# Modulation blocks behind their bank's products, bias rows loaded at a pair's start, and one product step ahead of the second group's scores

## The chip, the cores and the metric

One core of a Trainium2 chip runs the kernel as one program. The metric is the device time of one execution in microseconds (us). Engines: TensorE (PE in the profile, PEld its weight loads), VectorE (DVE), ScalarE (ACT), GpSimd (POOL) and SyncE (SP), which here issues nearly all DMAs.

## The reference

One layer of a hybrid diffusion model over T = 640 tokens (512 of a sample on an 8 by 64 grid, 128 of a prompt), width 1024:

```python
q_a, k_a, v_a, q_b, k_b, v_b = project(modulate(rmsnorm(x), shift, scale), w_in)
o_a = neighborhood_attn(q_a, k_a, v_a, cache_a_k, cache_a_v, rpb)      # 8 heads, 8x16 window, bias rpb
o_b = window_attn(rope_2d(q_b), rope_2d(k_b), v_b, cache_b..., sink)   # 8 heads, 2 kv heads
x = x + gate1 * rmsnorm(concat(rmsnorm(o_a), rmsnorm(o_b)) @ w_out)
x = x + gate2 * rmsnorm(conv_ffn(modulate(rmsnorm(x), shift2, scale2)))
shift, scale, gate1, shift2, scale2, gate2 = split(silu(c) @ w_mod + b_mod, 6)
```

This is a shortened form. The prompt's tokens attend to each other in full with the same weights, and their keys and values are outputs too. The modulation is 48 column blocks of 128: 24 of them are wanted only after attention.

## The kernel before, in words

All products are made of float32 operands split into a high and a low part, so each product of 128 by 128 weights is three matmuls (`mm3`, all recorded at line 127, in `mm`). In the same way `tt` (L111) stands for all two-operand passes and `act` (L108) for all passes of ACT.

**Stages.** Norms, transposes, the first modulation columns and V run to about 64 us in an order written by hand. From there to about 343 us the attention runs, and in that region a scheduler of the tile framework orders each engine's instructions from its own cost estimates; the source only gives the order of the program. Then the output projection and the feed-forward follow, by hand again.

**The attention region.** A software pipeline, `Pipe.slot` (L872), takes a list of jobs: for each of four head pairs p four tiles of neighbourhood attention and one of the prompt, then for each of four groups g the window attention. A job makes scores in a bank `psS` (two banks), a softmax (`soft1`, L620: a DVE pass at L626 adds the bias table `tab` and finds the extreme `nm`, writing a tile `P`; ACT takes the exponent), transposes of P (`psT`) and products with V (`psO`). Between the jobs' steps `fill_run` (L855) lets PE work on projections that a later job needs, for so many us as it is given: `qk_gen` (L584) makes query and key of the next pair, `qb_gen` (L1008) the rotated query of the next group, `kb_gen` and `vb_gen` the window's key and value.

**A bank and its block.** Each projection goes through `tgemm` (L542): 24 products of 128 x 320 (8 steps k of three) gather in columns 0 to 320 of a bank `psg`; there are two such banks. Columns 320 to 450 hold one modulation block at the same time, made by `side_gen` (L824) in four stages: (1) eight matmuls with a block of 128 columns of `w_mod`, tile `wms` (L371, in `ada_mm`); (2) a copy T by ACT, and `side_load` (L817), which starts the next `wms` of 512 KB on SP's queue into the one buffer there is; (3) a product of T with `sel` on PE (L835), which sums four row groups; (4) DVE adds the bias and puts the column into S, G or another table. 24 blocks go with 24 banks. What reads a finished bank (q, k, the rotation) is put on the list `pend`, and `flush` (L537) emits it at k = 1 of the next `tgemm`.

**Bias tables.** The relative-position bias of a head is loaded in four DMAs from a scratch tensor (`load_traw`, L242, on SP's queue) into a tile `traw`, from which POOL copies seven pieces into `tab` (`tab_ops`, L490, recorded at L505). `traw` and the P tiles are of one pool with eight buffers (L59). `pre_natten(p)` (L1180) puts the loads and the copies of the next pair's two heads on `bg`, a list from which each slot takes four entries. SP also loads the projection weights (`wst`, L338) and the cached keys and values (`cc`, L442 and L443), whose buffers come from a pool that the outgoing prompt keys (`ko`) use as well.

**Before the windows.** `pre_window(g)` (L1195) empties the fill list and puts the next group's query on it; the slots have 4.4 us each for the pairs and 4.2 for the groups.

Of the kernel before, what the change touches and what calls it, by code (L numbers as in the profile page):

```python
# [26 lines left out]
def trunk_kernel(  # L27
# [46 lines left out]
    def U(shape, name, dt=F32):  # L74
        return up_.tile(shape, dt, tag="u", name=name)
# [8 lines left out]
    def PB(shape, name, dt=F32):  # L84
        return pp_.tile(shape, dt, tag="p", name=name)
# [4 lines left out]
    def QT(shape, name, dt=F32):  # L90
        return qp_.tile(shape, dt, tag="q", name=name)
# [9 lines left out]
    def PS(kind, name):  # L101
        return PSB[kind].tile([128, 512], F32, tag=kind, name=name)
# [19 lines left out]
    def split(hi, lo, src):  # L122
        act(hi, src)
        tt(lo, src, f(hi), ALU.subtract)
# [4 lines left out]
    def mm3(out, lh, ll, rh, rl, start, stop):  # L129
        mm(out, lh, rh, start, False)  # L130
        mm(out, lh, rl, False, False)
        mm(out, ll, rh, False, stop)
# [109 lines left out]
    def load_traw(h):  # L242
        traw[h] = t = PB([128, 2, 256], f"traw{h}")
        for v in range(2):
            for jj in range(2):
                sv = scr[v, h]
                nc.sync.dma_start(
                    out=t[jj * 64:jj * 64 + 64, v, :],
                    in_=bass.AP(tensor=sv.tensor, offset=sv.offset + jj * 8, ap=[[32, 8], [1, 8], [1, 256]]))
# [130 lines left out]
    def hh(k, lo, s):  # L380
        return (hL if lo else hH)[k // 4][:, k % 4, s]
# [150 lines left out]
        for h_, l_, s_ in parts:  # L532
            tt(l_, s_, f(h_), ALU.subtract)

    pend = []

    def flush():  # L537
        now, pend[:] = pend[:], []
        for fn in now:
            fn()  # L540

    def tgemm(w, ch):  # L542


        wh, wl = w
        ps_ = PS("g", "psg")
        s_ = slice(ch * 320, ch * 320 + 320)
        sd = side_gen(ps_[:, 320:450], m128)
        yield next(sd, 0.0)
        for k in range(KD):  # L550
            mm3(ps_[:, 0:320], wh[:, k, :], wl[:, k, :], hh(k, 0, s_), hh(k, 1, s_), k == 0, k == KD - 1)
            if k == 1:
                flush()
            if ch and k == 3 and stream.nt > 1:
                stream.split()
            yield 0.41 + (next(sd, 0.0) if k in (2, 7) else 0.0)
        pend.append(lambda: next(sd, 0.0))
        return ps_

    RW = [slice(0, 64), slice(64, 128)]  # L560
# [23 lines left out]
    def qk_gen(p):  # L584
        q = QT([128, 2, T], f"q{p}", F32R)
        if p:
            load_cc(p)
        cc = CC.pop(p)
        w = stream.take()
        ps0 = yield from tgemm(w, 0)  # L590
        pend.append(lambda: split(q[:, 0, 0:320], q[:, 1, 0:320], ps0[:, 0:320]))
        ps1 = yield from tgemm(w, 1)
        pend.append(lambda: split(q[:, 0, 320:640], q[:, 1, 320:640], ps1[:, 0:320]))
        ku = U([128, 2576], f"k{p}", F32R)
        kt = ku[:, 0:2304].rearrange("p (e c) -> p e c", e=2)
        vc = ku[:, 2304:2560].rearrange("p (h s d) -> p h s d", h=2, s=2)
        QK[p] = (q, kt, vc)

        def part(o, src):
            n = src.shape[-1]  # L600
            return kt[:, 0, o:o + n], kt[:, 1, o:o + n], src

        w = stream.take()
        pt = PS("t", "pst")
        nc.tensor.transpose(pt[:, 0:128], cc[:, 0], ident)
        pend.append(lambda: k_ctx(kt, pt[:, 0:128], 448, 3))
        pend.append(lambda: split(vc[:, :, 0, :], vc[:, :, 1, :], cc[:, 1].rearrange("p (h d) -> p h d", h=2)))
        ps2 = yield from tgemm(w, 0)
        pend.append(lambda: splits(part(128, ps2[:, 0:320]), part(576, ps2[:, 192:320])))
        ps3 = yield from tgemm(w, 1)  # L610

        def last():
            splits(part(704, ps3[:, 0:192]), part(1024, ps3[:, 192:320]))
            nc.vector.tensor_copy(cc[:, 2], ps3[:, 192:320])
            pend.append(lambda: prompt_k_out(cc[:, 2], nak[:, p * 128:p * 128 + 128]))

        pend.append(last)
# [206 lines left out]
    def side_gen(ps_, m_, ahead=True):  # L824
        if not sides:
            return
        cb, w = sides.pop(0)
        what, k = cb // 8, cb % 8
        ada_mm(ps_, lambda k_: w[:, k_, :], 0, 128)
        yield 0.5  # L830
        act(m_, ps_[:, 0:128])
        if ahead:
            side_load()
        yield 0.0
        nc.tensor.matmul(ps_[:, 128:130], m_, sel[:, 0:2], start=True, stop=True, skip_group_check=True)  # L835
        yield 0.11
        bb = T1[:, W_MODT + cb:W_MODT + cb + 1].to_broadcast([128, 2])
        if what == 3:
            tt(S2[:, k, :], ps_[:, 128:130], bb, ALU.add)
        else:  # L840
            tmp = SM([128, 2], "gtmp")
            tt(tmp, ps_[:, 128:130], bb, ALU.add)
            if what == 4:
                ts(G2[:, k, :], tmp, 1.0, T1[:, W_GF + k:W_GF + k + 1], ALU.add, ALU.mult)
            else:
                gc = (W_GMP if what == 2 else W_GFP) + k
                ts((G1 if what == 2 else S1)[:, k, :], tmp, T1[:, gc:gc + 1], None, ALU.mult)
        yield 0.0
# [6 lines left out]
    def fill_run(us, last=None):  # L855

        carry[0] += us
        while fill and carry[0] > 0:
            try:
                d = next(fill[0][1])  # L860
                if d is None:
                    break
                carry[0] -= d
            except StopIteration:
                name = fill.pop(0)[0]
                if last is not None and name == last:
                    break
        carry[0] = min(carry[0], 0.0)

    bg = []  # L870
# [56 lines left out]
    def rope(src, o, n, dH, dL):  # L927

        mask = [i ^ 16 for i in range(32)]
        rx = FP([128, 2, 320], "rx")  # L930
        x_, sh = rx[:, 0, 0:n], rx[:, 1, 0:n]
        tt(x_, src, cs[:, 0, o:o + n], ALU.mult)
        nc.vector.stream_shuffle(sh, src, mask)
        tt(sh, sh, cs[:, 1, o:o + n], ALU.mult)
        tt(x_, x_, sh, ALU.add)
        js = slice(o // 64, (o + n) // 64)
        split(jview(dH)[:, js], jview(dL)[:, js], x_.rearrange("p (j r c) -> p j r c", r=8, c=8))
# [70 lines left out]
    def qb_gen(g):  # L1008
        q = QB[g] = QT([128, 2, T], f"qb{g}", F32R)
        w = stream.take()  # L1010
        p0 = yield from tgemm(w, 0)
        dH, dL = q[:, 0, 0:512], q[:, 1, 0:512]
        pend.append(lambda: rope(p0[:, 0:320], 0, 320, dH, dL))
        p1 = yield from tgemm(w, 1)

        def last():
            rope(p1[:, 0:192], 320, 192, dH, dL)
            split(q[:, 0, 512:640], q[:, 1, 512:640], p1[:, 192:320])

        pend.append(last)  # L1020
# [97 lines left out]
    def run_ops(ops):  # L1118
        for fn in ops:
            fn()  # L1120
# [59 lines left out]
    def pre_natten(p):  # L1180
        def run():
            fill_run(1e9)
            flush()
            if p < 3:
                fill.append((f"qk{p + 1}", qk_gen(p + 1)))
                for h in (2 * p + 2, 2 * p + 3):
                    bg.append(lambda h=h: load_traw(h))
                    bg.extend(tab_ops(h, (nc.gpsimd,)))
            else:
                fill.append(("kb", kb_gen()))  # L1190
                fill.append(("vb", vb_gen()))
                fill.append(("qb0", qb_gen(0)))
        return run

    def pre_window(g):  # L1195
        def run():
            fill_run(1e9)
            for _ in range(4 if g == 0 else 1):
                flush()
            if g == 0:  # L1200
                ob_.extend(U([128, 4, T], f"ob{i}", F32R) for i in range(2))
            if g == 2:
                wa[0, 0], ops = load_wo(0, 0, 0, wr_, 0)
                bg.extend(ops)
            if g == 3:
                wa[0, 1], ops = load_wo(0, 0, 1, wr_, 0)
                run_ops(ops)
                for i in range(2):
                    wa[1, i], ops = load_wo(0, 1, i, None, 0)
                    bg.extend(ops)  # L1210
            if g < 3:
                fill.append((f"qb{g + 1}", qb_gen(g + 1)))
            else:
                fill.append(("wa0", wa_gen(0)))
        return run
# [784 lines left out]
```

## Time and profile before

| | us |
|---|---|
| median of 3 runs (848.74 to 855.26) | 848.97 |
| profiled execution | 855.52 |
| its span | 853.6 |
| PE busy | 806.5 (94%) |
| DVE, ACT, POOL busy | 564.7, 436.0, 303.2 |
| mean granted clock of TensorE | 0.976 |

A row of the page names a line, an engine, an operation and its tiles, out<-in. In a row of the timeline the bracket at the end holds the idle time just before the instruction and what ended it. A row of the waits gives an engine, its tile and line, what it waited for, the total, the count and the longest. The granted clock is the share of full speed that TensorE was allowed in a stretch.

### The profile page before, as it was taken

How to read it: one execution, taken by the hardware profiler on the slowest of the kernel's cores; microseconds unless marked ns; L12 is line 12 of the kernel's file. 1: busy time of each engine (PE TensorE's matmuls, PEld its weight loads, DVE VectorE, ACT ScalarE, POOL GpSimd, SP SyncE). 2: the span in 40 equal slices, each digit the busy share in tenths (PEclk: the TensorE clock that was granted, in tenths of full speed). 3: DMA queues.
4: the chain of work that ended last, by engine and by line, in shares of the span. 5: the costliest groups of instructions: out<-in, count | busy, mean ns of one | idle time of the engine just before them, and what ended most of it. 6: DMA issues, size and time to landing. Idle time of an engine off the chain costs nothing.

```text
span 853.6 us, 13902 instructions
## 1 busy us (share of the span) xinstructions
PE 806.5 (94%) x5304; PEld 708.5 (83%) x5304; DVE 564.7 (66%) x1023; ACT 436.0 (51%) x876; POOL 303.2 (36%) x352
## 2 busy tenths in 40 slices
PE   6999989899999999989997999999999999999996
PEld 5679778788777777768997999999999987888885
DVE  3455555555888875676679899898898864332115
ACT  5345665645667886465445545546456544332112
POOL 3452333323221211346964466575575200000002
PEclk8999999999999999999998999999999999999999
DMA  9954535436312113567124243233332436434313
GB/s 290 277 142 127 155 97 142 122 105 164 86 50 75 50 51 104 197 207 196 42 65 128 83 129 110 87 115 104 107 115 84 125 114 221 171 110 161 114 50 124
DMA packets 140158, 106.59 MB, mean 125 GB/s; under 512 B 12560, under 2 KB 121388, under 8 KB 140092
## 3 DMA queue, kind: packets, MB, share of 16 engines
q1 hardware_dynamic: 139084, 105.05, 41.5%
q8 instruction: 42, 0.69, 0.4%
q10 hardware_dynamic: 1008, 0.66, 0.3%
q14 instruction: 24, 0.20, 0.1%
HBM read 92.53 MB, written 13.16 MB: 124 GB/s over the span
## 4 chain that ended last, share of the span: by engine, by line
PE 48%; DVE 28%; ACT 7%; DMA 5%; issue 4%; POOL 4%; SPq 1%; DVEq 0%; ACTq 0%; POOLq 0%
PE psd L127 16%; PE psg L127 8%; DVE cv L120 7%; DVE ou L111 5%; PE psv L127 4%; DVE cv L111 3%; DVE owl L111 3%; PE zx L127 3%; POOL fg L111 3%; PE psya L127 3%; PE psyb L127 2%; DMA wms<-in_w_mod_dram 2%; PE psS L127 2%; ACT cv L108 2%; DVE yy L111 2%
## 5 line engine op out<-in xcount | busy, mean ns | idle before, releaser
L127 PE MATMUL psd<-dwh,a 128*128 128x512 f32 x440 | 138.3, 395 | 0.0
L111 POOL TENSOR_TENSOR wsum<-wraw 128x512 f32<-128x512 f32 x36 | 77.2, 2166 | 96.9 <-DVE oc L111 89.1
L127 PE MATMUL zx<-h2H,ou 128*128 128x322 f32 x392 | 96.7, 316 | 7.5 <-DVE cv L120 4.4
L127 PEld LDWEIGHTS psd<-dwh,a 128*128 128x128 f32 x440 | 82.9, 188 | 19.7
L127 PE MATMUL psd<-dwl,a 128*128 128x512 f32 x220 | 87.1, 396 | 0.1
L111 DVE TENSOR_TENSOR dwl<-wd,dwh 128x1024 fp32r<-128x1024 f32 x22 | 26.9, 1224 | 86.7 <-ACT dwh L108 86.7
L127 PE MATMUL psg<-hH,wh 128*128 128x320 f32 x224 | 76.0, 339 | 4.4 <-ACT T L108 4.2
L127 PEld LDWEIGHTS zx<-h2H,ou 128*128 128x128 f32 x392 | 69.0, 192 | 9.9 <-DVE yy L111 5.2
L127 PE MATMUL psg<-hH,wl 128*128 128x320 f32 x224 | 70.5, 315 | 0.0
L127 PE MATMUL psg<-hL,wh 128*128 128x320 f32 x224 | 70.3, 314 | 0.0
L108 ACT ACTIVATE dwh<-wd 128x1024 fp32r<-128x1024 f32 x22 | 23.3, 1060 | 91.4 <-PE psd L127 85.7
L117 POOL TENSOR_SCALAR rdv<-ssdc 128x1 f32<-128x1 f32 x5 | 1.6, 329 | 177.3 <-ACT jk L108 177.3
L127 PE MATMUL zx<-h2L,ou 128*128 128x322 f32 x196 | 61.4, 313 | 0.0
L127 PEld LDWEIGHTS psg<-hH,wh 128*128 128x128 f32 x224 | 42.8, 191 | 13.2 <-ACT T L108 7.9
L108 ACT ACTIVATE cv<-yy,T 128x642 f32<-128x642 f32 x20 | 17.7, 886 | 66.1 <-DVE yy L111 66.1
L127 PEld LDWEIGHTS psd<-dwl,a 128*128 128x128 f32 x220 | 41.3, 188 | 10.4 <-DVE dwl L111 0.6
L111 POOL TENSOR_TENSOR wl<-wst,wh 128x1024 fp32r<-128x1024 f32 (+1 forms) x12 | 27.7, 2311 | 58.5 <-ACT wh L108 41.7
L120 DVE SCALAR_TENSOR_TENSOR cv<-yy,T,cv 128x641 f32<-128x641 f32 x40 | 35.4, 884 | 17.9 <-ACT cv L108 17.2
L108 ACT ACTIVATE P<-P,nm 128x320 f32<-128x320 f32 (+3 forms) x64 | 40.3, 630 | 7.0 <-DVE nm L626 6.9
L127 PEld LDWEIGHTS psg<-hL,wh 128*128 128x128 f32 x224 | 43.1, 192 | 0.5
L127 PEld LDWEIGHTS psg<-hH,wl 128*128 128x128 f32 x224 | 42.9, 192 | 0.0
L108 ACT ACTIVATE cv<-cv 128x642 f32<-128x642 f32 x22 | 16.4, 744 | 50.2 <-DVE cv L120 50.2
(354 smaller groups left out, 2248.0 us busy)
## 6 DMA issues: line engine op xcount, KB each, us to landing
wraw<-in_w_up_dram SPq DMA_DIRECT2D x40, 512.0 KB
wms<-in_w_mod_dram SPq DMA_DIRECT2D x32, 512.0 KB
wd<-in_w_down_dram SPq DMA_DIRECT2D x22, 512.0 KB
wm<-in_w_mod_dram SPq DMA_DIRECT2D x16, 512.0 KB
aD<-cv SPq DMA_DIRECT2D x22, 321.0 KB
ar<-aD SPq DMA_DIRECT2D x11, 642.0 KB
wst<-in_w_in_dram SPq DMA_DIRECT2D x10, 512.0 KB
yD<-Y SPq DMA_DIRECT2D x5, 512.0 KB
```

Source lines behind the costliest of these rows:

```text
L108: return nc.scalar.activation(out=out, in_=in_, func=func, **kw)
L111: return (eng or nc.vector).tensor_tensor(out=out, in0=a, in1=b, op=op)
L117: return e.tensor_scalar(out=out, in0=a, scalar1=s1, scalar2=s2, op0=op0, op1=op1)
L120: return nc.vector.scalar_tensor_tensor(out=out, in0=a, scalar=s, in1=b, op0=op0, op1=op1)
L127: return nc.tensor.matmul(out, l, r, start=start, stop=stop, skip_group_check=True, **kw)
```

## The change

Three edits, all in the attention region. New lines shift the numbers below the first one by up to six: the sel product is L835 before and L841 after, `side_load`'s DMA L821 and L827, the transposes L708 and L714.

1. `tgemm` makes its block's eight matmuls behind its 24 products instead of ahead of them. The copy T goes on `pend` (so it is emitted at k = 1 of the next `tgemm`, as the first reader of the bank, together with the next `wms` load), sel comes at k = 4 of the next `tgemm`, and DVE's bias add is put on `pend` there. The last block's rest is emitted in `pre_window(3)`.
2. `pre_natten` calls `load_traw` for both heads of the next pair at once, at the start of the pair; only the copies stay on `bg`.
3. `pre_window(0)` runs the fill list for 2.0 us more right after the second group's query has been put on it.

```diff
 def tgemm(w, ch):
     sd = side_gen(ps_[:, 320:450], m128)
-    yield next(sd, 0.0)
     for k in range(KD):
         mm3(ps_[:, 0:320], ...)
         if k == 1:
             flush()
...
-        yield 0.41 + (next(sd, 0.0) if k in (2, 7) else 0.0)
+        late = 0.0
+        if k == 4 and side_late:
+            late = next(side_late[0], 0.0)
+            pend.append(lambda g=side_late.pop(): next(g, 0.0))
+        yield 0.41 + late
+    yield next(sd, 0.0)
     pend.append(lambda: next(sd, 0.0))
+    side_late.append(sd)
     return ps_
...
 def pre_natten(p):
             for h in (2 * p + 2, 2 * p + 3):
-                bg.append(lambda h=h: load_traw(h))
+                load_traw(h)
                 bg.extend(tab_ops(h, (nc.gpsimd,)))
...
 def pre_window(g):
+            if g == 3:
+                for g_ in side_late:
+                    next(g_, 0.0)
+                    next(g_, 0.0)
...
             if g < 3:
                 fill.append((f"qb{g + 1}", qb_gen(g + 1)))
+                if g == 0:
+                    fill_run(2.0)
```

How the scheduler's order moves. On PE, at the second block (hH and hL are the split activations, wh and wl the split weights, k_872 and q_807 the pair's keys and queries); before:

```order
L127 MATMUL psg<-hH_573,wl 128x320
L835 MATMUL psg<-sel,T_99 128x2
L127 MATMUL psS<-k_872,q_807 128x384 x3
L371 MATMUL psg<-wms,cpad 32x128 x8
L127 MATMUL psg<-hH_174,wh 128x320
L127 MATMUL psg<-hL_175,wh 128x320
L127 MATMUL psg<-hH_174,wl 128x320
```

and now, at the first and the second block:

```order
L127 MATMUL psg<-hH_573,wl 128x320
L371 MATMUL psg<-wms,cpad 32x128 x8
L127 MATMUL psg<-hH_174,wh 128x320
L127 MATMUL psg<-hL_175,wh 128x320
L127 MATMUL psg<-hH_174,wl 128x320
L127 MATMUL psS<-k_872,q_807 128x384 x6
...
L127 MATMUL psg<-hH_573,wl 128x320
L841 MATMUL psg<-sel,T_99 128x2
L127 MATMUL psg<-hH_573,wh 128x320
...
L371 MATMUL psg<-wms,cpad 32x128 x8
L127 MATMUL psS<-k_872,q_807 128x384 x6
```

The sel product stood at its bank's end, next to the following block; now it stands 15 products behind the block, in the following bank, with 9 more products from there to the next block. The group of six scores, which was split into three and more, stands whole. In the whole region PE changes from one kind of work to another 273 times, 306 before. Of the 24 sel products none carried a wait before; now 14 carry one for DVE and 17 one for ACT. Of the products of psg 26 waited for ACT and 3 for DVE; now it is 2 and 24.

On SP's queue, from the first pair on; before:

```order
L247 DMA traw_984<-scr 64x1x256 x4
L821 DMA wms<-in_w_mod_dram 128x8x128
L338 DMA wst<-in_w_in_dram 128x8x128 x2
L821 DMA wms<-in_w_mod_dram 128x8x128
L442 DMA cc<-in_cache_a_k_dram 128x128
L443 DMA cc<-in_cache_a_v_dram 128x128
L442 DMA cc<-in_cache_a_k_dram 128x128
L443 DMA cc<-in_cache_a_v_dram 128x128
L338 DMA wst<-in_w_in_dram 128x8x128
L821 DMA wms<-in_w_mod_dram 128x8x128
L247 DMA traw_1135<-scr 64x1x256 x4
```

and now:

```order
L247 DMA traw_975<-scr 64x1x256 x4
L827 DMA wms<-in_w_mod_dram 128x8x128
L247 DMA traw_981<-scr 64x1x256 x4
L338 DMA wst<-in_w_in_dram 128x8x128 x2
L442 DMA cc<-in_cache_a_k_dram 128x128
L443 DMA cc<-in_cache_a_v_dram 128x128
L442 DMA cc<-in_cache_a_k_dram 128x128
L827 DMA wms<-in_w_mod_dram 128x8x128
L338 DMA wst<-in_w_in_dram 128x8x128
L443 DMA cc<-in_cache_a_v_dram 128x128
L827 DMA wms<-in_w_mod_dram 128x8x128
```

The second head's rows (traw_1135, now traw_981) stood behind four cache loads and now stand ahead of all of them; the second `wms` load stood ahead of the cache loads and now stands behind three of them.

On PE, before the first scores of the windows (kvU the window's keys, qb_2645 and qb_2638 the rotated query); before:

```order
L835 MATMUL psg<-sel,T_99 128x2
L995 MATMUL pstb<-ident,vbT 128x128
L708 MATMUL psT<-ident,P 128x128 x3
L371 MATMUL psg<-wms,cpad 32x128 x8
L127 MATMUL psg<-hH_174,wh 128x320
...
L127 MATMUL psg<-hH_174,wl 128x320
L127 MATMUL psS<-kvU,qb_2645 128x384 x6
L708 MATMUL psT<-ident,P 128x128 x3
```

and now:

```order
L127 MATMUL psg<-hH_573,wl 128x320
L841 MATMUL psg<-sel,T_99 128x2
L714 MATMUL psT<-ident,P 128x128 x4
L127 MATMUL psS<-kvU,qb_2638 128x384 x6
L714 MATMUL psT<-ident,P 128x128 x2
L127 MATMUL psg<-hH_573,wh 128x320
```

Nine products of the second group's query stood between the last block and the window's first scores, and now fifteen stand between the last projection and these scores, with sel behind them; nine more products follow before the next block, and the transposes of P, six in all, are four ahead and two behind.

More of the change, by code (lines that the diff above doesn't have):

```diff
@@ L533, in splits @@
             tt(l_, s_, f(h_), ALU.subtract)
-    pend = []
+    pend, side_late = [], []
     def flush():
```

## The prediction

> **What bounds the kernel now.** I read the busy times first, then the table of stretches, the waits of TensorE (PE), the chain that ended last, and single rows around each wait.
>
> ```profile
> PE 806.5 (94%) x5304; PEld 708.5 (83%) x5304; DVE 564.7 (66%) x1023; ACT 436.0 (51%) x876; POOL 303.2 (36%) x352
> PE   6999989899999999989997999999999999999996
> ```
>
> PE sets the end: busy for 806.5 of 853.6 us, and nearly full in every slice. Moving work on another engine pays only where PE stood idle for it. All three edits lie between 64 and 343 us. The next view sums the waits of PE from 78 to 330 us (line, what it waited for, us in total, times, longest).
>
> ```profile
> PE psg L127 <- ACT T L108: 4.2, 7, 1.1
> PE psS L127 <- DVE nm L626: 3.0, 2, 1.5
> PE psg L371 <- DMA wms<-in_w_mod_dram: 2.1, 3, 0.8
> PE psS L127 <- ACT qb L108: 1.8, 1, 1.8
> ...
> PEld psg L127 <- ACT T L108: 7.9, 14, 1.4
> ```
>
> These four groups of PE, 4.2 + 3.0 + 2.1 + 1.8 = 11.1 us, are what the change can touch. PEld counts the first of them as 7.9, because a weight load starts its wait while the matmul ahead still runs. Two stretches hold something more than waiting (columns: length, busy of PE, PEld, DVE, ACT, POOL, granted clock, DMA share, GB/s):
>
> ```profile
> 117.00:122.60 5.60, 4.14 (x42) 3.28 (x37) 2.78 (x9) 3.07 (x9) 2.37 (x6) 1.00 0.62 140
> 122.60:127.00 4.40, 3.89 (x16) 3.00 (x17) 2.26 (x8) 2.34 (x8) 1.75 (x6) 0.64 0.01 2
> 127.00:150.00 23.00, 23.00 (x191) 19.95 (x190) 12.65 (x45) 14.18 (x39) 8.44 (x19) 0.99 0.50 135
> 150.00:156.10 6.10, 4.63 (x47) 3.75 (x45) 2.41 (x7) 3.22 (x8) 2.22 (x6) 1.00 0.61 131
> 156.10:161.00 4.90, 4.20 (x21) 3.89 (x22) 3.56 (x13) 3.80 (x12) 3.52 (x8) 0.69 0.00 0
> ```
>
> After each of the two stalls that end at 122.6 and 156.1 the granted clock is 0.64 and 0.69 for more than 4 us; between them it is 0.99. So such a stall costs its idle time and then some.
>
> **Part A, the bias rows of two heads loaded first.** The stall can be followed back, POOL and DVE first, then PE, then the SP queue, then the chain:
>
> ```profile
> 121.67 0.29 POOL L505 COPY tab<-traw 64x128 f32<-64x128 f32 x1 [0.85 <-DMA traw<-scr]
> 122.00 0.56 DVE L626 CUSTOM_DVE_ANT_0 P<-psS,tab 128x384 f32<-128x384 f32 x1 [2.05 <-POOL tab L505]
> 122.62 0.41 PE L127 MATMUL psS<-k,q 64*128 64x320 f32 x2 [1.48 <-DVE nm L626]
> 156.12 0.70 PE L127 MATMUL psS<-k,q 64*128 64x320 f32 x5 [1.49 <-DVE nm L626]
> 113.94 0.34 SPq L442 DMA_DIRECT2D cc<-in_cache_a_k_dram  x1
> 115.93 2.44 SPq L247 DMA_DIRECT2D traw<-scr  x4
> 109.86 4.01 DMA out_dram<-ko
> 116.58 2.96 DMA traw<-scr
> ```
>
> The store of ko holds the cache load at 113.94, the odd head's bias rows are queued behind that on SP, and POOL copies them last. DVE's score pass writes a P tile from the same eight buffers as traw, so it starts only when that copy has been read, at 122.00; PE has no free score bank until then. These bias rows belong to a later pair: nobody needs them yet, only their buffer. Loaded at the pair's start they stand ahead of the cache loads on SP, as the order shows, so none of their four DMAs waits for ko, and the copies are done some slots earlier. What goes: 5.60 − 4.14 = 1.46 idle, 3.89 × (1 − 0.64) = 1.40 of clock, 6.10 − 4.63 = 1.47 idle, 4.20 × (1 − 0.69) = 1.30 of clock; together −5.6. The gaps inside the slow stretches, 4.40 − 3.89 and 4.90 − 4.20, are left to part B. What could be late next is a P tile behind another buffer of that pool. Bounds: −5.6 if both stalls go, 0 if P still finds its buffer taken. I take −5.6.
>
> **Part B, the blocks behind the products.** A block is 16 passes at line 371, a copy T on ACT, and a product with sel. Today the block opens its bank, T and sel are due inside the same 24 products, and PE waits for T:
>
> ```profile
> 88.88 0.42 PE L127 MATMUL psg<-hH,wh 128*128 128x320 f32 x1 [0.29 <-ACT T L108]
> 157.51 0.41 PE L127 MATMUL psg<-hH,wh 128*128 128x320 f32 x1 [0.68 <-ACT T L108]
> 193.13 0.41 PE L127 MATMUL psg<-hH,wh 128*128 128x320 f32 x1 [1.13 <-ACT T L108]
> ```
>
> Afterwards T is copied while the next bank's products run, and no product waits behind it in its own bank: −4.2 by the waits of PE (bounds 0, if the wait moves whole, and −7.9, by PEld). The work itself is the same 192 block matmuls and 24 sel products.
>
> The sel product gets a wait in its place. T now stands first on ACT among what the bank's end releases, and in the order 17 sel products wait for ACT and 14 for DVE. Queued behind sel on PE is everything, so its slack counts. Rows of the banks, and the pace of products:
>
> ```profile
> L108 ACT ACTIVATE T<-psg x24: 254/277/286, 81.4 to 283.0; 128x128 f32<-128x128 f32 x24
> L108 ACT ACTIVATE q<-psg x8: 415/421/437, 67.8 to 163.6; 128x320 fp32r<-128x320 f32 x8
> L111 DVE TENSOR_TENSOR q<-psg,q x8: 492/492/493, 68.2 to 164.1; 128x320 fp32r<-128x320 f32 x8
> 64.19 7.06 PE psg L127 x48
> ```
>
> 48 products in 7.06 us are 0.147 each. In the tightest place sel comes 15 products, 2.2 us, after the block's end; T 0.28, then q on ACT 0.42 and on DVE 0.49 are 1.19. Idle queues give no wait; a busy DVE does. I take +1.5 (bounds 0, and 4.2, the whole wait of today). Changes of kind of work on PE fall from 306 to 273 in this region, since score groups are split less; a sel alone instead of beside a block costs about as much as an unsplit group saves. I put that at 0; the extra delay of a sel was at most 0.1 us, so ±1.
>
> **Part D, the blocks' weight loads.** One buffer, 512 KB: the next load starts when a block is done, and the next block can come no sooner than it lands.
>
> ```profile
> 79.72 6.00 DMA wms<-in_w_mod_dram
> 86.17 0.33 SPq L442 DMA_DIRECT2D cc<-in_cache_a_k_dram  x1
> 85.85 0.64 PE L371 MATMUL psg<-wms,cpad 128*32 128x128 f32 x16 [0.85 <-DMA wms<-in_w_mod_dram]
> 79.02 0.64 PE L371 MATMUL psg<-wms,cpad 128*32 128x128 f32 x16
> 84.18 0.28 PE L835 MATMUL psg<-sel,T 128*128 128x2 f32 x2
> 163.13 0.37 SPq L821 DMA_DIRECT2D wms<-in_w_mod_dram  x1
> 168.22 0.64 PE psg L371 x16
> 220.48 0.83 PE L127 MATMUL psS<-kvU,qb 64*128 64x384 f32 x6 [1.83 <-ACT qb L108]
> ```
>
> The load goes out 79.72 − 79.02 = 0.70 after its block's start and lands 5.1 (163.13 to 168.22, no wait there) to 6.1 (79.72 to 85.85) later, so blocks can follow each other every 5.8 to 6.8 us. The new order spaces most of them wider. Between the first two lie 24 products, one sel and six scores: 24 × 0.147 + 0.65 + 0.21 + 0.83 = 5.2, so PE waits 0.6 to 1.6; the load also stands behind one more cache load on SP, which today went out at 86.17. The first block, 24 products later than at 79.02, starts at about 82.6 and would let its successor's load go at 83.4, so that costs up to 2.8 more. Two later pairs have nothing between but 24 products and sel, 4.4: 1.4 to 2.4 each. Sum 3.4 to 9.2. I take 4.5, near the low end, since the load at 163.13, in a quieter stretch, is the nearest row for the two later pairs, and the cache load may go out earlier too. Less the 2.1 of today: +2.4 (bounds +1.3 and +7.1).
>
> [...]
>
> **Part C, products ahead of the second group's scores.** The window's first scores waited for the rotated query:
>
> ```profile
> 220.06 0.36 ACT L108 ACTIVATE qb<-rx 128x192 fp32r<-128x192 f32 x1 [2.46 <-DVE rx L111]
> ```
>
> That is the 1.83 at 220.48. The order now has 15 products there instead of 9, 6 × 0.147 = 0.9 more work, and the block that stood there stands elsewhere. The products are taken from a later slot, and group 0 has fewer of them beside its transposes. Bounds −1.8 and 0; I take −1.0, the middle.
>
> **Sum**, against the profiled execution, 855.52 us (span 853.6 and 1.9 around it): −5.6 − 4.2 + 1.5 + 2.4 − 1.0 = −6.9, so 848.6 for it. The runs' median is 848.97, 6.55 below the profiled execution, with one of three runs at 855.26. What the profiled one lost I can't see in the others; if part of it is granted clock, A is smaller in the median, −2.9 (its idle time) instead of −5.6. I carry the difference: 848.97 − 6.9 = **842.0 us**. This case's own range: 837 (A and B whole, D +1.3, C −1.8, sel +0.5) to 846 (A without the clock, B −4.2, D +4.5, C 0).
>
> **Rivals.**
>
> First, all four waits go and none replaces them: −5.6 − 4.2 − 1.8 − 2.1 = −13.7, 835.3 us. For it: the load landed in time at 168.22, and most blocks are spaced wider than 6 us. Against it: the pairs at 4.4 us are shorter than any load shown. [...] Chance 0.25.
>
> Second, slower: the weight loads become the bound. Blocks then follow at the pace of the loads, and a bank can't be finished without its block.
>
> ```profile
> 109.86 0.53 SPq L821 DMA_DIRECT2D wms<-in_w_mod_dram  x1
> 116.86 0.64 PE L371 MATMUL psg<-wms,cpad 128*32 128x128 f32 x16 [0.43 <-DMA wms<-in_w_mod_dram]
> 203.56 0.65 PE L371 MATMUL psg<-wms,cpad 128*32 128x128 f32 x16
> ```
>
> One load took 7.0, from 109.86 to 116.86. The seventeenth block, at 203.56, would stand 24 products later without any gain, at 207.1; from 82.6 that is 16 spacings of 7.8 us. So this decides from loads above 7.8 − 0.7 = 7.1 us in the mean. At 7.3 the spacing is 8.0 and the seventeenth block stands at 210.6, +3.5, with sel +1.5: 848.97 + 5.0 = 854 us. Against it: of the loads shown only one came near that. Chance 0.08.
>
> Third, the early load doesn't free the P tile in time, since traw stays in the same eight buffers: A is 0, and −4.2 + 1.5 + 2.4 − 1.0 = −1.3 gives 847.7 us. For it: buffers are handed out in turn, so a tile that is asked for earlier also takes a turn earlier, in front of other P tiles, and five of DVE's passes into P tiles still carry a wait for such a load and POOL's copy of it in the new order. Against it: no cache load stands ahead of those loads on SP any more. Chance 0.17.
>
> **How the numbers follow.** Forecast 0.50, rivals 0.25, 0.08, 0.17. The range 834 to 850 holds the forecast, the first and the third, and leaves out most of the second and a tail below. About what a measurement here can tell from no change is 1%, 8.5 us: faster means below 840.5. That is most of the first rival (0.20) and a quarter of the forecast (0.13): 0.33. Slower than 857.5 needs the second rival with loads longer still: 0.03. The rest, 0.64, is within 1%.
>
> **What would show it.** A right: no wait of DVE's score pass for POOL's copies, and a clock near 1.0 right through from 117 to 161. B right: PE's wait for T near 0, waits on sel up to 1.5 us in sum. D right: PE's waits at line 371 about 4.5, at the second block and at two later ones. C right: no wait of 1.8 us ahead of the window's first scores. I am wrong if the clock still falls in that part, if line 371 waits more than 8 us, or if P waits for a buffer elsewhere.

## The result and the profile after

The change makes the kernel slower. Before: 851.55 us, median of 15 runs (847.29 to 855.26); after: 856.57 us, median of 15 (852.60 to 862.98). The ratio is 1.0068, 95% interval 1.0043 to 1.0094. Forecast were 842.0 us and a range of 834 to 850.

Over the whole span PE is busy for the same time as before; what it waits for has changed (page and waits of PE, 78 to 340 us, of the kernel after):

```profile
PE 807.3 (94%) x5304; PEld 711.2 (83%) x5304; DVE 564.5 (66%) x1023; ACT 436.3 (51%) x876; POOL 302.4 (35%) x352
...
PE psT L1050 <- DVE pwL L111: 5.3, 5, 2.1
PE psg L371 <- DMA wms<-in_w_mod_dram: 5.1, 3, 4.5
PE pst L611 <- DVE ptL L111: 2.6, 2, 1.7
PE psS L127 <- DVE nm L632: 1.5, 2, 0.8
PE psg L841 <- DVE qb L111: 0.9, 1, 0.9
```

The waits for T are gone, and so are the two stalls that the bias rows made. In their place stand 5.3 us for pwL (the low part of the split P, which DVE makes from the bank of transposes), 2.2 before, and 5.1 us for the blocks' weights, 2.1 before. Where the time turns is seen from two milestones. The window's first scores came at 220.48 before; in the kernel after they come here:

```profile
213.51 0.79 PE L127 MATMUL psS<-kvU,qb 64*128 64x384 f32 x6
```

That is 7.0 us earlier, with six more products and one block fewer done by then. The four products of the output projection that come next after the attention, though, start 3.8 us later; before, then after:

```profile
324.76 1.09 PE L127 MATMUL psya<-wo,oa 128*128 128x512 f32 x4
```

```profile
328.57 1.09 PE L127 MATMUL psya<-wo,oa 128*128 128x512 f32 x4
```

So the window groups, between these two, take 104.3 us before and 115.1 after: 10.8 us are lost there, more than was won in the pairs. Of the 10.8, 4.4 are more idle time of PE (3.7 before, 8.1 after) and 6.4 longer busy time (100.6 before, 106.9 after), at a mean granted clock of 0.98 and 0.90. The stretches of that part (length, busy of PE, PEld, DVE, ACT, POOL, granted clock, DMA share, GB/s), before, then after:

```profile
225.00:250.00 25.00, 23.29 (x180) 20.37 (x180) 20.95 (x67) 17.22 (x48) 6.39 (x13) 0.93 0.22 64
250.00:275.00 25.00, 24.28 (x179) 19.70 (x177) 21.90 (x74) 19.87 (x55) 4.27 (x11) 1.00 0.21 64
275.00:300.00 25.00, 24.30 (x154) 19.15 (x155) 21.91 (x73) 20.16 (x52) 4.99 (x11) 1.00 0.15 43
300.00:325.00 25.00, 24.41 (x139) 18.80 (x140) 18.77 (x53) 20.43 (x50) 4.06 (x7) 1.00 0.25 64
```

```profile
225.00:250.00 25.00, 23.36 (x158) 19.05 (x156) 17.59 (x63) 17.67 (x49) 6.59 (x13) 0.80 0.14 43
250.00:275.00 25.00, 22.13 (x164) 18.84 (x162) 20.54 (x70) 18.27 (x50) 4.20 (x10) 0.93 0.21 64
275.00:300.00 25.00, 22.00 (x136) 18.02 (x129) 19.96 (x66) 17.97 (x48) 4.89 (x11) 0.86 0.28 85
300.00:325.00 25.00, 24.40 (x128) 18.47 (x127) 16.16 (x43) 18.02 (x41) 4.07 (x7) 0.93 0.09 25
```

PE idles 8.1 of these 100 us instead of 3.7. Busy time times the missing clock is 11.0 us instead of 1.6. That estimate is too high, since the busy time between the milestones grew by only 6.4 us; either way this item is the larger one.

One end of a group shows how it comes about. Group 1 before, then after, on PE:

```profile
264.71 0.98 PE L1044 MATMUL psT<-ident,P 128*128 128x128 f32 x7
265.63 0.64 PE L371 MATMUL psg<-wms,cpad 128*32 128x128 f32 x16
266.20 0.41 PE L127 MATMUL psg<-hH,wh 128*128 128x320 f32 x1
...
267.19 0.49 PE L1044 MATMUL psT<-ident,P 128*128 128x128 f32 x3
```

```profile
258.42 0.64 PE L371 MATMUL psg<-wms,cpad 128*32 128x128 f32 x16
258.99 0.55 PE L127 MATMUL psS<-kvU,qb 64*128 64x128 f32 x6
259.47 1.09 PE L1050 MATMUL psT<-ident,P 128*128 128x128 f32 x8
262.67 1.57 PE L1050 MATMUL psT<-ident,P 128*128 128x128 f32 x6 [2.11 <-DVE pwL L111]
```

Before, a block and six products lay between the transposes while DVE read the bank out (pwL); the three transposes at 267.19 wait for nothing. Now the block ends the bank ahead of the scores, the next bank's products come only behind the transposes, and PE stands 2.11 us. The six transposes behind the stall already take 1.57 us, 0.26 each, against 0.14 in the row above them.

The other new stall is in the pairs (SP, the chain, PE; of the kernel after):

```profile
125.97 2.66 SPq L247 DMA_DIRECT2D traw<-scr  x4
128.75 0.38 SPq L827 DMA_DIRECT2D wms<-in_w_mod_dram  x1
128.75 7.15 DMA wms<-in_w_mod_dram
135.95 1.08 PE L371 MATMUL psg<-wms,cpad 128*32 128x128 f32 x16 [4.47 <-DMA wms<-in_w_mod_dram]
```

### The profile page after: what moved, and what is told of

Its sections match the earlier page's. It is cut to its first block, busy times and chain, and to the rows that moved or that the text cites. A ratio compares the mean times of both kernels' runs of the same rounds, so it can differ in the third digit from the quotient of the medians.

```text
span 855.7 us, 13905 instructions
## 1 busy us (share of the span) xinstructions
PE 807.3 (94%) x5304; PEld 711.2 (83%) x5304; DVE 564.5 (66%) x1023; ACT 436.3 (51%) x876; POOL 302.4 (35%) x352
## 4 chain that ended last, share of the span: by engine, by line
PE 52%; DVE 27%; ACT 7%; issue 4%; POOL 4%; DMA 4%; SPq 0%; DVEq 0%; ACTq 0%; POOLq 0%
PE psd L127 18%; PE psg L127 8%; DVE cv L120 6%; DVE ou L111 5%; PE psv L127 4%; PE zx L127 4%; DVE owl L111 3%; DVE cv L111 3%; PE psya L127 3%; POOL fg L111 3%; DMA wms<-in_w_mod_dram 3%; PE psO L127 3%; PE psS L127 2%; PE psyb L127 2%; DVE yy L111 2%
```

## The experiments

My theory after the result (T): the moved blocks leave PE without other work at the ends of the window groups, and the clock falls behind each such stall (in the kernel after it is 0.57 and 0.58 in the 4 us behind the two of 2.11 us). Rivals: the early rows hold up the weight loads (U), the extra 2.0 us of products rob group 0 (V), DVE's pace rules the windows anyway (W). In the tables, clock is the mean over all runs of a kernel; before's is 0.979 to 0.982.

**The parts alone.** Each undoes the other parts of the change.

```diff
 e1: only the tgemm / side_late edits and the rest of the last block
 e2: only   -bg.append(lambda h=h: load_traw(h))   +load_traw(h)
 e3: only   +if g == 0: fill_run(2.0)
 e4: e1 and e2 together
```

> Only the modulation blocks are moved behind their bank's products; rows and fill as before. Theory T (the ends of the window groups lose their cover: in the new order six scores and fourteen transposes stand on PE with no product among them, PE waits there for DVE's pwL and the clock falls after it): slower than before by 3 to 8 us, with two waits of psT for pwL of about 2 us and a granted clock near 0.6 behind each. Rival U (the second head's early rows hold up the weight load of a block on SP): without the early rows the blocks alone are faster by 2 to 5 us.

> Only the bias rows are loaded at the pair's start. Theory T: faster by 3 to 6 us, since the two waits of DVE's score pass for POOL's copy and the low clock behind them are gone and nothing else moves. Rival U: the loads hold up blocks' weight loads here too, and the time is the same or up to 4 us slower, with a wait above 3 us at the blocks.

> Only the 2.0 us of products ahead of the second group's scores. Theory T: within 2 us of before, the 1.8 us wait ahead of the window's first scores gone. Rival V (these products are the cover that group 0 lacks later): slower by 3 us or more, with new waits of PE between 225 and 245 us and a lower clock there.

> Blocks and rows moved, without the 2.0 us of products. Theory T: slower than before by 2 to 6 us, much like the whole change; the waits in the ends of groups 1 and 2 stay. Rival V: the same as before or faster, since the products taken out of group 0 are back.

| | median us | ratio to before, 95% interval | clock |
|---|---|---|---|
| e1 blocks | 859.13 | 1.0120 (1.0075 to 1.0165) | 0.969 |
| e2 rows | 850.37 | 0.9986 (0.9960 to 1.0012) | 0.982 |
| e3 fill | 853.42 | 1.0041 (1.0013 to 1.0070) | 0.977 |
| e4 blocks and rows | 857.69 | 1.0083 (1.0054 to 1.0113) | 0.971 |
| the change | 856.57 | 1.0068 (1.0043 to 1.0094) | 0.970 |

The blocks alone cost 8.8 us by the medians and 10 by the ratio (6 to 14; one of six runs, 868.19, stands far above the others), more than T expected, with 7.0 us of waits for pwL. U falls as the main cause: a wait of 3.44 us at the block near 135 us is in e1 too, without the early rows. In e4, which has them, it is 3.74, in the change 4.47, so they add between 0.3 and 1.0 us.

e3 is a miss for T: the products alone make the kernel about 3.5 us slower (1.1 to 6.0), and the wait that they were to remove is still there:

```profile
215.59 0.44 PE L127 MATMUL psS<-kvU,qb 64*128 64x384 f32 x1 [1.81 <-ACT qb L108]
```

In e1 and e4, without these products, it is gone; a transpose just ahead of the scores waits 1.0 us for DVE there. So it was the moved blocks that removed it. V's mechanism isn't seen either: from 225 to 250 us the only wait of PE in e3 is one of 0.20 us, at 234.82, and the clock of the 4 us behind it is 1.00. Why e3 is slower stays open. As e4, without the products, is no faster than the change, V falls as the main cause.

The rows bring nothing that can be told from no change, though in the profile of e2 both stalls are gone: there T, too, expected too much. In e1, with the rows loaded late as before, PE doesn't wait for them either (its first wait for nm comes at 223.00, in the windows): each of the two edits alone frees PE of these stalls. What e2 still shows is one longer wait for a block:

```profile
161.34 0.65 PE L371 MATMUL psg<-wms,cpad 128*32 128x128 f32 x16 [1.56 <-DMA wms<-in_w_mod_dram]
```

**The blocks moved only where no window tail follows.** The banks of the three later queries open with their block as before (its T copied at k = 5 where a late sel is still due).

```diff
-def tgemm(w, ch):
+def tgemm(w, ch, late_=True):
+    if not late_: yield next(sd, 0.0)
...
+        if not late_ and k in (k2, 7): late += next(sd, 0.0)
...
+ qb_gen: tgemm(w, 0, g == 0), tgemm(w, 1, g == 0); no fill_run(2.0)
```

> Blocks behind their products in the banks of the pairs, of the window's key and value and of the first rotated query; in the banks of the three later queries the block opens its bank as before. Rows early, no extra 2.0 us. Theory T (the uncovered ends of the window groups cost the time, by idle and above all by the clock that falls after them): no wait of psT for pwL above 1.9 us and at most one near 1.7 as before; the clocked part of the span (span times granted clock) stays at 829 to 832, what the clock takes goes back from 25 to 16 to 19 us, so 846 to 850 us, 0 to 0.5% faster than before. Rival U (the blocks' weight loads and the early rows in the pairs cost it): still slower than before by 4 us or more.

850.20 us, ratio 1.0004 (0.9984 to 1.0025), clock 0.978. In the profile the granted clock is 1.00 in each of the seven stretches of 4 us that begin with a wait of PE in the windows, from 228.03 to 314.94, and 7 us of e4 are back. The gain over before that T allowed isn't there: the wait near 136 us is 4.29 us and stays.

**More products left for the ends.** The same blocks as in the change, with less fill per window slot, so that the products lie later.

```diff
-        us = 4.2 if g < 3 else 8.4
+        us = 3.4 if g < 3 else 8.4
```

> The whole change, and the fill of a window slot 3.4 instead of 4.2 us for groups 0 to 2, so that products of the next query lie later; in the order products and a block then stand between the transposes at the ends of groups 1 and 2. Theory T: the two waits of 2.1 us for pwL are gone or below 1 us, the clock stays up behind them, and the time is 3 to 7 us below that of the change, near before's. Rival W (the tails' products don't matter; DVE's pace sets the window part): the same as the change within 2 us, with the waits moved to other instructions of PE.

849.36 us, ratio 0.9994 (0.9974 to 1.0014), clock 0.980. The waits for pwL are no longer among the larger ones, and two of the stretches read:

```profile
250.00:275.00 25.00, 24.49 (x178) 19.44 (x179) 21.96 (x77) 18.79 (x52) 1.85 (x8) 1.00 0.22 64
275.00:300.00 25.00, 24.09 (x159) 19.12 (x158) 19.99 (x64) 19.65 (x50) 4.50 (x12) 1.00 0.29 86
```

One number cures the windows (clock 1.00 in both, 0.93 and 0.86 in the change), and W falls.

**Useless work in the gaps.** Two tries to keep PE busy without giving it anything to gain; 28 products that nobody reads are added to the change.

```diff
+for n_ in range(14 if sk in (1, 2) else 0):
+    mm(hv[n_ % 2][:, 256:512], hh(n_ % 8, 0, slice(0, 128)), hh(n_ % 8, 0, slice(0, 256)), True, True)
```

> The whole change with useless work added: 14 products of 256 columns, whose result nobody reads, after the prompt's scores of groups 1 and 2, where PE waits 2.1 us for pwL. They add about 3 to 4 us of PE work. If it is the clock that the idle costs, the stretches behind those two waits run at a clock near 1.0 and the time falls by 2 to 6 us below the change though PE does more. If only the idle itself counts, the time is that of the change, within 1 us, or up to 2 us longer.

> The whole change with 14 useless products of 256 columns right behind the prompt's scores of groups 1 and 2, this time free to run at once, ahead of the transposes that wait 2.1 us for pwL. If the clock is what idle costs: the two waits fall below 0.6 us, the clock behind them stays near 1.0, and the time is 2 to 6 us below the change though PE does some 3.6 us more. If only the idle counts: the time of the change within 2 us, since work takes the place of waiting.

e7: 858.47 us, 1.0085 (1.0052 to 1.0117); e9: 857.68 us, 1.0063 (1.0038 to 1.0088). Neither covers the gap. In e7 those of group 2 themselves waited (and in group 1 the transposes ahead of them, 1.69 us); in e9 they ran at once, but a shorter wait came behind them (e7, then e9):

```profile
287.29 3.07 PE L127 MATMUL psS<-hH 128*128 128x256 f32 x14 [2.55 <-ACT P L108]
```

```profile
258.23 1.91 PE L127 MATMUL psS<-hH 128*128 128x256 f32 x14
263.17 0.55 PE L1052 MATMUL psT<-ident,P 128*128 128x128 f32 x3 [1.49 <-DVE pwL L111]
```

So this question, clock or idle alone, was not settled by them.

**The blocks' weight loads on ACT's queue.**

```diff
-            nc.sync.dma_start(out=w, in_=wmod...)
+            nc.scalar.dma_start(out=w, in_=wmod...)
```

> The whole change with the blocks' weight loads issued by ACT's queue instead of SP's, so that they stand behind no cache load, bias row or projection weight. If the order on SP made the 4.5 us wait at the block near 136 us, that wait falls to 1 to 2.5 us (two blocks there are 4.4 us apart and the load takes 5 to 6) and the time to 1 to 4 us below the change. If the transfer itself is what takes long (shared with the bias rows), the wait stays above 3.5 us and the time is the same.

859.11 us, 1.0103 (1.0062 to 1.0143). The load went out at 127.71, 1.0 us earlier, and landed 7.4 us later all the same:

```profile
127.71 0.37 ACTq L827 DMA_DIRECT2D wms<-in_w_mod_dram  x1
135.15 1.08 PE L371 MATMUL psg<-wms,cpad 128*32 128x128 f32 x16 [3.31 <-DMA wms<-in_w_mod_dram]
```

The wait is 3.31 us, between the two outcomes that were named, and the time is no better. The order on SP is then about a quarter of that stall, 1.2 of 4.5 us, or less: in e9, whose pairs are those of the change, the same wait is 3.80. The rest is a long transfer, with bias rows and a projection weight on their way, asked for by a block that comes too soon. The distance alone doesn't make the stall: in the kernel after, the second of the two close pairs of blocks, at 163.26 and 167.79, had no wait, since the load went out right behind the first, at 163.96, and was there within 3.8 us.

**Blocks further apart: a square.** With 5.2 us of fill in a pair's slot instead of 4.4 the two closest pairs of blocks are 5.8 us apart in place of 4.4 (5.81 and 5.87 in the profile of e10; 4.53 at 163.26 and 167.79 in the kernel after).

```diff
-    us = 4.4 if p < 3 else 7.2
+    us = 5.2 if p < 3 else 7.2
```

> The whole change, 3.4 us of fill in a window slot and 5.2 instead of 4.4 in a pair's slot, which puts the two pairs of blocks that were 4.4 us apart to 5.8 in the order. If the short distance to the next weight load makes the 4.2 us wait near 136 us, that wait falls to about 2.8 or less, and the time to 2 to 5 us below that with 3.4 alone, 844 to 848 us, faster than both kernels. If the wait stays above 3.5 us the transfer starts later too, and the time is that with 3.4 alone.

> The kernel before with 3.4 instead of 4.2 us of fill in a window slot and nothing else: a control. If 3.4 only mends what the moved blocks did, this is within 2 us of before. If 3.4 is better in itself, it is 3 us or more faster than before, and what it gained on the change is not a cure of the change's own fault.

> The whole change with 5.2 instead of 4.4 us of fill in a pair's slot, and the window slots left at 4.2: the fourth corner of a square with the change, 3.4 alone and both. If the two faults are separate (blocks too close to each other in the pairs, ends without cover in the windows), the wait near 136 us is gone, the two waits of 2.1 us for pwL stay, and this is 2 to 5 us below the change and 5 to 9 us above the kernel with both numbers. If 5.2 is what makes that kernel fast, this is already within 3 us of it.

| ratio to before | pairs 4.4 | pairs 5.2 |
|---|---|---|
| windows 4.2 | 1.0068 (the change) | 1.0003 (0.9982 to 1.0025) |
| windows 3.4 | 0.9994 (e6) | 0.9932 (0.9904 to 0.9960) |

Each number takes off 0.6 to 0.7%, with the other or without it: the two gains add up, as those of two separate faults would. With both, e10, the kernel takes 846.35 us (843.15 to 849.05) and beats both kernels. The wait near 136 us is gone altogether, which is more than the 1.4 us of extra distance: the load no longer goes out behind the bias rows (127.56 in e10, with the rows from 128.02 on, and the block at 132.66 finds it there). From 125 to 150 us e10 reads

```profile
125.00:150.00 25.00, 25.00 (x229) 22.11 (x228) 15.31 (x53) 15.85 (x46) 10.54 (x28) 1.00 0.49 135
```

In e12 the two waits for pwL stand as before the cure (2.11 and 2.09 us), as expected:

```profile
256.57 1.57 PE L1050 MATMUL psT<-ident,P 128*128 128x128 f32 x6 [2.11 <-DVE pwL L111]
283.86 1.57 PE L1050 MATMUL psT<-ident,P 128*128 128x128 f32 x6 [2.09 <-DVE pwL L111]
```

The control, e11, takes 854.63 us, 1.0040 (1.0014 to 1.0065), a little slower than the 2 us allowed: 3.4 is no gain in itself, so it mends what the moved blocks did. For 5.2 there is no such control. The wait near 136 us goes with it, but how much 5.2 would bring to the kernel before is not known, and with it how much of the 0.7% below before belongs to the change.

## Why the prediction was wrong

The sign was wrong. It came from what the sum left out, less from its terms.

- **What held.** B: the waits for T are gone, and the new waits of sel are 0.9 and 0.4 us where 1.5 was forecast. D: 5.1 us of waits at line 371 against 4.5, though 4.47 of it in one place, and none at the second block.
- **What came out by luck.** C's 1.8 us wait is gone, but by the moved blocks (e1, e4) and not by the products (e3), and half of it stands close by: the 0.9 us of sel are at 212.70, just ahead of these scores. Up to the window's first scores 7.0 us are won, close to the sum of −6.9, but not by its terms. From 78 us to these scores PE is idle for 9.8 us where it was 10.3, since new stalls (4.47 for the weights, 2.6 of transposes of cached keys for ptL) took the place of the old ones; its busy time fell from 132.2 to 125.7. Most of that lies with the scores of the pairs, whose groups now stand whole. Of the 64x384 form, before, then after:

```profile
L127 PE MATMUL psS<-k,q 64*128 64x384 f32 x48 | 9.3, 399 | 0.0
```

```profile
L127 PE MATMUL psS<-k,q 64*128 64x384 f32 x48 | 6.3, 368 | 0.0
```

  It is 9.3 us in every profiled kernel whose blocks all open their bank (before, e2, e3, e11) and 6.3 to 6.9 in the others. The prediction had put the unsplit groups at 0, give or take 1.
- **The step that failed** stands in part B: "The work itself is the same", with the moved order of kinds of work put at 0. The order was read for the pairs and the first window scores only. A bank's block and the products of the next bank were the cover for DVE at the ends of the window groups, where DVE is busy 21 of 25 us; nothing in the sum priced their leaving, though part C named it for group 0. What the runs showed: the window groups take 10.8 us longer, e1 puts the edit at about +10 us, and e5 and e6 take some 7 us of it away again by edits of the window part alone. That six scores and fourteen transposes stood there with no product between could have been read in the order.
- **The clock was counted on one side.** The prediction booked 2.7 us of clock as won and none for the new stalls. The 4.47 us stall was followed by this, in the kernel after:

```profile
135.90:140.00 4.10, 4.05 (x31) 3.30 (x32) 1.84 (x8) 1.52 (x5) 3.55 (x5) 0.50 0.44 130
```

  Part D's +2.4 left this out, and it was too small: in e12, where the stall is gone, the time is 5.5 us lower by the ratios, as far as that isn't a gain of 5.2 in itself. The mean granted clock is 0.981 before (25 runs) and 0.970 after (15). That is at most 1.1% of 850, 9 us, of which part is idle time anyway; the whole loss is 5 to 6 us. The size of this share is not shown apart from the idle that comes with it, since the fillers failed.
- **A was mis-sized**: −5.6 forecast, in e2 −1.2 us (interval −3.4 to +1.0). The stalls went, but a new 1.56 us wait for a block came, and the 2.7 us of clock were those of one execution: before's profiled one had a clock of 0.976, below the mean of its runs, and in e11's the same two stalls last 0.60 and 1.21 us and are followed by a clock of 1.00. As the moved blocks free PE of these stalls too (e1), A and B also counted partly the same time.
- **The rivals.** The second one had the right side and half the mechanism: blocks too close for their loads. Its price was put at a mean over sixteen loads; it was one spacing with one load of 7.15 us. The case's own lower bound, 837, doesn't follow from the terms named with it, which give 839.2 with B at −4.2 and 835.5 with B at −7.9. Of the loads of 512 KB, one took 3.8 us at most (out at 163.96), and two took 7.15 and 7.4 us (on SP's queue, and on ACT's in e8, with bias rows and a projection weight on their way).

## What to carry to other kernels

When an edit moves work on a full engine, look for every place from which the work leaves, above all where that work hid another engine; a scheduler's cost table can make such places far from the edit. Price each new stall with the clock behind it (here 0.50 to 0.62 behind 17 of 18 waits of 2 us or more), and take the clock's loss from several executions, not from the one that was profiled. After such a move the numbers that spread the filler work have to be chosen anew: here two of them turned +0.7% into −0.7%, the second without a control.

## What the runs showed of the hardware

In the 14 profiled executions, from 78 to 330 us, I took each wait of PE and the granted clock of the 4 us behind it. Of 18 waits of 2 us or more, 17 were followed by a clock of 0.50 to 0.62, and one of 2.32 us in e1 by 1.00; of 38 waits between 1 and 2 us, 14 by one under 0.9. One and the same wait, 1.8 us ahead of the window's first scores, was followed by 1.00 in three kernels (before, e2, e11) and by 0.77 in e3. So a short stall of one length was followed by a low clock in one profiled execution and not in another. The shortest of these waits with a clock of 0.50 behind it was 1.29 us, at 290.82 in e8. What sets the clock was not shown.

The spread of the times goes with the clock: before's runs reach from 845.35 to 857.26 us, and in each set of runs the time mostly rises as the mean granted clock falls, from 843.5 us of span at 0.988 to 852.7 at 0.975 in one set of 25.
